# Layer 1's state mixer: chunk recurrence by one folded transition matrix per chunk, in place of three products per chunk

## The chip, the cores and the metric

One Trainium2 chip, one core of it. The metric is the device time of one execution in microseconds (us). A core has a matrix engine (TensorE, PE in the profile; its weight loads are PEld), a vector engine (DVE), a scalar engine (ACT), a general engine (POOL) and an engine that here only issues DMAs (SP). Each works through its own queue in order; they meet by semaphores that the compiler framework sets from the tiles that instructions read and write.

## The reference, cut to what matters

A backbone of two layers over 256 context and 256 latent tokens of 1024 features. Each layer is a feed-forward block, a token mixer and a feed-forward block. The mixer of layer 1 is the RWKV-7 recurrence, in both directions, over 16 heads of 64 features:

```
def step(s, inp):                        # s: state (64 x 64) of one head and direction
    r_t, w_t, k_t, v_t, kk_t, a_t = inp
    sa = einsum('ebhvk,ebhk->ebhv', s, -kk_t)
    s = s * w_t[..., None, :] + sa[..., None] * (kk_t * a_t)[..., None, :] + v_t[..., None] * k_t[..., None, :]
    return s, einsum('ebhvk,ebhk->ebhv', s, r_t)
s_fin, ys = lax.scan(step, s0, xs)
y = ys[:, 0] + jnp.flip(ys[:, 1], axis=0)
```

The context is scanned first, its readouts are not needed; the latent tokens are scanned from its final state. The summed readouts pass a normalization per head, a bonus and a gate, and the output projection.

## The kernel before, in words

The 512 tokens are cut into 8 chunks of 64 (0 to 3 context, 4 to 7 latent), the heads into four sets `s` of four heads: two feature tiles `q` of 128 features, each with two heads `par` in its two halves of 64 partitions. Directions are `d` = 0, 1. Within a chunk the recurrence becomes matrix algebra: a strictly triangular 64 x 64 matrix per chunk and head has to be inverted, and the state crosses the chunk by products.

The work on a set is written as generators:

- `prep` (L1513 ff., with `factors` and `scores`): rates, decay factors (L1596), the scaled operands `bk` and `zs` (L1601 to L1611), the scores as products (L1655, L1658), masked by DVE (L1660 to L1663), and transposes (L1669).
- `invert`: one transposition of all diagonal 32 x 32 blocks (tile `inva`, L1690), then an elimination of 31 steps on DVE, a multiplication (L1712) and a subtraction (L1715) each; in between `rebase` on POOL (L1681) multiplies `zs` by decays, and `modulation` computes a part of the next block's conditioning (L1756, L1765). At its end transpositions back (L1690) and two rounds of 32 x 32 products that join the blocks (L1733, L1741, evicted L1735, L1743). This end is called the inverse tail below.
- `recur`: the chain over 8 chunks, both directions in step. A chunk is a product of state and `zs` (L1798), an eviction by ACT (L1802), a product by the inverse (L1813), an eviction with sign (L1815), a product by `bt` (L1822) and on DVE the addition of the decayed state `f` (L1827; the decay is POOL's, L1793). The latent chunks add readouts (L1807, L1834, L1838 to L1843).
- `output` (normalization, bonus, gate; L1853 to L1903), and for the last set `early_o` and `late_o` (the output projection).

`together` interleaves generators by their share of steps done, and the order written so is the order in each queue. In `run`, set 0's inversion goes together with set 1's preparation, set 0's chain with set 1's inversion; then the chain of set `s` together with preparation and inversion of set `s + 1`; the last chain together with `early_o`. `output(s)` follows each chain. Tiles of one name share a buffer: a new one waits until the last reader of the old one is done.

Of the kernel before, what the change touches and what calls it, by code (L numbers as in the profile page):

```python
# [15 lines left out]
T = 512  # L16
# [1126 lines left out]
def consts_wkv():  # L1143


    p = np.arange(128)
    tau, j = p[:, None], np.arange(65)[None, :]
    cum = [((tau // L) == ch) * ((tau % L < j).astype(np.float32) - (tau % L < L // 2)) for ch in range(2)]
    blk = ((p[:, None] // L) == (p[None, :] // L)).astype(np.float32)
    oh = np.zeros((128, 8, 16), np.float32)  # L1150
    for f in range(8):
        oh[p, f, 2 * f + p // L] = 1.0
    s, t = (p % L)[:, None], np.arange(L)[None, :]
    masks = [(s < t), (s <= t)]
    return np.concatenate(cum + [np.eye(128) - blk / L, blk, oh.reshape(128, 128)] + masks, 1).astype(np.float32)
# [60 lines left out]
class Mixer1:  # L1216
# [15 lines left out]
    def run(self, epi):  # L1232
# [6 lines left out]
        with K.ctx_stack() as c2:  # L1239
# [12 lines left out]
            self.chain = [[self.cbank().rearrange("p (a b c) -> p a b c", a=4, b=2), K.bank((4, 2, 64), long=True)] for _ in range(2)]  # L1252
# [22 lines left out]
    def with_first(self, st, recur, prep, n):  # L1275

        def run():
            for i, _ in enumerate(prep):
                if i == 8:
                    self.loads(st)  # L1280
                    next(recur)
                yield
        return run(), n


    def consts(self):
        nc, mp, i, K = self.nc, self.mp, self.ins, self.K
        cw = mp.tile([128, 642], F32, name="cw")
# [4 lines left out]
        self.masks = cw[:, 514:642]  # L1293
# [174 lines left out]
    def values(self, pool):  # L1468

        K, nc = self.K, self.nc  # L1470
        for hf in range(2):
# [8 lines left out]
            st = pool.tile([128, 4 * T], F32, tag=f"sv{hf}", name="st")  # L1480
# [10 lines left out]
    def state(self, s, pool):  # L1491
# [76 lines left out]
    def factors(self, st, q, d, w2, a2):  # L1568
        K, nc, g = self.K, self.nc, self.late if d and self.late else self.g
        ZS, FX = st["ZS"], st["FX"]  # L1570

        for par in range(2):
            nc.gpsimd.memset(ZS[par][half(1 - par), d, q], 0.0)
# [25 lines left out]
        BK = g.tile([128, 8, 3, 64], F32, tag="bk", name="bk")  # L1599
        st["BK", d] = BK  # L1600
        nc.vector.scalar_tensor_tensor(out=BK[:, :, 0, :], in0=c8(TA[:, d]), scalar=0.5, in1=U[:, :, 1:65], op0=ALU.mult, op1=ALU.mult)  # L1601
        nc.vector.tensor_tensor(out=BK[:, :, 1, :], in0=c8(KD[:, d]), in1=U[:, :, 1:65], op=ALU.mult)
        nc.scalar.copy(out=BK[:, :, 2, :], in_=BK[:, :, 0, :])
        ctx = lambda z: z[:, d, q, 0:256].rearrange("p (c t) -> p c t", t=64)
        lat = lambda z: z[:, d, q, 256:768].rearrange("p (c x) -> p c x", x=128)
        c0, l0 = (slice(n, n + 4) for n in pos)
        for par in range(2):
            p = half(par)
            nc.gpsimd.tensor_tensor(out=lat(ZS[par])[p, :, 64:128], in0=c8(r)[p], in1=W[p, l0, 1:65], op=ALU.mult)
            nc.vector.tensor_tensor(out=lat(ZS[par])[p, :, 0:64], in0=c8(kk)[p, l0], in1=W[p, l0, 0:64], op=ALU.mult)  # L1610
            nc.vector.tensor_tensor(out=ctx(ZS[par])[p], in0=c8(kk)[p, c0], in1=W[p, c0, 0:64], op=ALU.mult)  # L1611
        yield

        fx = lambda n0, n1, i: nc.gpsimd.tensor_tensor(out=FX[:, d, q, n0:n1], in0=W[:, i:i + n1 - n0, 64], in1=U[:, i + 1:i + 1 + n1 - n0, 0],  # L1614
                                                       op=ALU.mult)
        if d == 0:
            fx(0, 7, 0)
        else:
            fx(0, 3, 4)
            fx(4, 7, 0)  # L1620
            nc.gpsimd.tensor_tensor(out=FX[:, d, q, 3:4], in0=W[:, 7:8, 64], in1=U[:, 0:1, 0], op=ALU.mult)
# [10 lines left out]
    def scores(self, st, q, d):  # L1632

        K, nc = self.K, self.nc
        ZS, BT, BR, FX, AB = (st[n] for n in ("ZS", "BT", "BR", "FX", "AB"))
        BK = st["BK", d]
        pos = [4, 0] if d else [0, 4]
        ctx = lambda z: z[:, d, q, 0:256].rearrange("p (c t) -> p c t", t=64)
        lat = lambda z: z[:, d, q, 256:768].rearrange("p (c x) -> p c x", x=128)

        bk = lambda c, par, p=slice(0, 128): BK[p, c, par:par + 2, :].rearrange("p a t -> p (a t)")
        u0 = d * 16 + q * 8

        def diag(par, u, ps):

            h0, h1 = (slice(64 * par + h, 64 * par + h + 32) for h in (0, 32))
            nc.scalar.copy(out=AB[h0, u:u + 4, :], in_=ps[h0, :, 0:64])
            nc.scalar.copy(out=AB[h1, u:u + 4, 0:32], in_=ps[h1, :, 32:64])

        mask = lambda a, x, n: self.masks[a, x].unsqueeze(1).to_broadcast([64, 4, n])  # L1650
        for par in range(2):
            p, o = half(par), half(1 - par)
            pl = K.bank((4, 128))
            for c in range(4):
                nc.tensor.matmul(pl[:, c, :], lhsT=bk(pos[1] + c, par), rhs=lat(ZS[par])[:, c, :], start=True, stop=True)  # L1655
            pc = K.bank((4, 128))
            for c in range(4):
                nc.tensor.matmul(pc[:, c, :], lhsT=bk(pos[0] + c, par), rhs=ZS[par][:, d, q, 64 * c:64 * c + 128], start=True, stop=True)  # L1658
            diag(par, u0 + 4, pl)
            nc.vector.tensor_tensor(out=lat(ZS[par])[o], in0=mask(o, slice(0, 128), 128), in1=pl[o], op=ALU.mult)  # L1660
            nc.vector.tensor_tensor(out=BR[p, d, q], in0=mask(p, slice(64, 128), 64), in1=pl[p, :, 64:128], op=ALU.mult)
            diag(par, u0, pc)
            nc.vector.tensor_tensor(out=ctx(ZS[par])[o], in0=mask(o, slice(0, 64), 64), in1=pc[o, :, 0:64], op=ALU.mult)  # L1663
            yield
        for par in range(2):
            p = half(par)
            pt = K.bank((7, 64))
            for c in range(7):
                nc.tensor.transpose(pt[:, c, :], bk(pos[c // 4] + c % 4, par, p), K.ident[p, p])  # L1669
            nc.scalar.copy(out=BT[par][:, d, q], in_=pt)  # L1670
            yield

    def rebase(self, st):

        for d in range(2):
            for q in range(2):
                for par in range(2):
                    p, z = half(par), st["ZS"][par]
                    for x, n, c in ((z[p, d, q, 64:256], slice(0, 3), 64), (z[p, d, q, 256:768], slice(3, 7), 128)):
                        x = x.rearrange("p (n c) -> p n c", c=c)  # L1680
                        self.nc.gpsimd.tensor_tensor(out=x, in0=x, in1=st["FX"][p, d, q, n].unsqueeze(2).to_broadcast([64, n.stop - n.start, c]), op=ALU.mult)  # L1681
                        yield

    @steps(38)
    def invert(self, st):
# [12 lines left out]
        for _, r1 in R:  # L1698
            nc.gpsimd.memset(AB[r1, :, 0:32], 0.0)
        yield  # L1700
        tmp = g.tile([128, 256], F32, tag="invt", name="invt")
        rebase, mods = self.rebase(st), self.modulation(5 + st["s"])
# [381 lines left out]
```

## Time and profile before

| | |
|---|---|
| time, three runs | 2631.14, 2634.19, 2635.12 us (median 2634.19) |
| the profiled execution | 2629.81 us, its span 2628.1 us |
| busy of the span | PE 93%, DVE 52%, ACT 42%, POOL 16% |
| state mixer from its first inversion to its last result | 1969.4 to 2411.7 us |

Times inside the span count from its start. "PEclk" is the clock that the chip granted to TensorE, as a share of full: 1.00 is 2.4 GHz, 0.50 is 1.2 GHz, and a figure between is a mean over a stretch that has both. A busy TensorE says that products are under way; at half clock the same products are busy for longer.

### The profile page before, as it was taken

To read this page: it belongs to the slowest core of one execution; us is meant where nothing else is said; L and a number is where in the kernel's file an instruction comes from. 1 tells how busy PE (TensorE), PEld (TensorE's weight loads), DVE (VectorE), ACT (ScalarE), POOL (GpSimd) and SP (SyncE) were. 2 spreads that over 40 slices of the span, in tenths; PEclk is the share of its full clock that TensorE was granted. 3 is DMA by queue.
4 is the path that set the end of the run, shared out by engine and by line. 5 is a ranking of instruction groups with operands and counts; after the bars stand their busy time and mean duration, and the time that the engine had idled before them with its cause. 6 is when DMAs were issued, how large, how long until landed. Compare 5 with 4: busy or idle time off the path is not lost. (4 is left out here: it accounts for less than half of the span.)

```text
span 2628.1 us, 39209 instructions
## 1 busy us (share of the span) xinstructions
PE 2441.9 (93%) x15555; PEld 1953.1 (74%) x15555; DVE 1363.5 (52%) x2406; ACT 1106.5 (42%) x2005; POOL 425.6 (16%) x546
## 2 busy tenths in 40 slices
PE   6999999998999999999999999997986888886998
PEld 5777777776777778777778888876875565655998
DVE  2322336775687473223244333356858867654555
ACT  4222225675565443222244222343644363534443
POOL 0000001033000110000010000023146273642000
PEclk9999999998999899999999999998998797967999
DMA  7545445343211234444444333323415312323553
GB/s 234 177 136 176 152 147 192 106 120 78 80 57 46 76 101 165 144 152 153 133 164 129 110 105 112 118 99 106 141 50 143 85 49 83 97 74 112 178 185 121
DMA packets 245476, 320.96 MB, mean 122 GB/s; under 512 B 34748, under 2 KB 186237, under 8 KB 245293
## 3 DMA queue, kind: packets, MB, share of 16 engines
q1 hardware_dynamic: 234157, 291.07, 35.3%
q0 software_dynamic: 7104, 20.05, 2.1%
q10 hardware_dynamic: 4032, 7.34, 0.8%
q8 instruction: 122, 2.00, 0.3%
q14 instruction: 61, 0.50, 0.1%
HBM read 301.77 MB, written 18.71 MB: 122 GB/s over the span
## 5 line engine op out<-in xcount | busy, mean ns | idle before, releaser
L62 DVE TENSOR_TENSOR wlo<-raw,whi 128x1024 fp32r<-128x1024 f32 x352 | 437.4, 1244 | 769.7 <-ACT whi L61 764.7
L420 PE MATMUL ps<-hth,whi 128*128 128x512 f32 (+1 forms) x1920 | 690.8, 362 | 28.2 <-ACT hth L397 13.1
L421 PE MATMUL ps<-htl,whi 128*128 128x512 f32 (+1 forms) x1920 | 687.3, 358 | 2.8 <-DVE htl L1344 2.8
L422 PE MATMUL ps<-hth,wlo 128*128 128x512 f32 (+1 forms) x1920 | 684.0, 357 | 0.0
L61 ACT CAST whi<-raw 128x1024 fp32r<-128x1024 f32 x352 | 368.9, 1049 | 680.2 <-PE ps L421 434.6
L420 PEld LDWEIGHTS ps<-hth,whi 128*128 128x128 f32 x1920 | 365.0, 191 | 101.8 <-issue 15.4
L421 PEld LDWEIGHTS ps<-htl,whi 128*128 128x128 f32 x1920 | 366.5, 191 | 56.7 <-issue 4.2
L422 PEld LDWEIGHTS ps<-hth,wlo 128*128 128x128 f32 x1920 | 366.3, 191 | 53.3 <-issue 2.8
L366 POOL TENSOR_SCALAR ss<-ss 128x1 f32<-128x1 f32 x42 | 22.2, 528 | 1441.1 <-ACT junk L364 1414.6
L420 PE MATMUL ps<-whi,g 128*128 128x512 f32 x616 | 244.0, 397 | 0.0
L421 PE MATMUL ps<-wlo,g 128*128 128x512 f32 x616 | 242.4, 394 | 0.0
L422 PE MATMUL ps<-whi,g 128*128 128x512 f32 x616 | 242.0, 394 | 0.0
L420 PEld LDWEIGHTS ps<-whi,g 128*128 128x128 f32 x616 | 116.3, 189 | 27.8 <-ACT whi L61 0.8
L422 PEld LDWEIGHTS ps<-whi,g 128*128 128x128 f32 x616 | 116.2, 189 | 26.9 <-DVE g L511 0.2
L421 PEld LDWEIGHTS ps<-wlo,g 128*128 128x128 f32 x616 | 116.3, 189 | 25.4
L510 ACT CAST g<-sg 128x512 fp32r<-128x512 f32 (+1 forms) x88 | 49.5, 565 | 109.2 <-DVE sg L507 109.2
L503 ACT ACTIVATE sg<-ps 128x512 f32<-128x512 f32 (+1 forms) x88 | 47.7, 542 | 102.6 <-PE ps L422 102.5
L507 DVE TENSOR_TENSOR sg<-sg,ps 128x512 f32<-128x512 f32 (+1 forms) x88 | 54.2, 618 | 39.1 <-PE ps L422 38.7
L1655 PE MATMUL ps<-zs,bk 128*128 128x128 f32 x256 | 42.2, 315 | 28.8 <-POOL fx L1614 17.5
L511 DVE TENSOR_TENSOR g<-sg,g 128x512 fp32r<-128x512 f32 (+1 forms) x88 | 54.4, 621 | 23.2 <-ACT g L510 23.2
L1655 PEld LDWEIGHTS ps<-zs,bk 128*128 128x128 f32 x256 | 36.9, 220 | 35.5 <-POOL fx L1614 18.6
L1712 DVE TENSOR_TENSOR invt<-inva,invx 128x110 f32<-128x110 f32 (+35 forms) x244 | 57.8, 275 | 1.9
(461 smaller groups left out, 3708.2 us busy)
## 6 DMA issues: line engine op xcount, KB each, us to landing
raw<-in_ffn_w_in_dram SPq DMA_DIRECT2D x176, 512.0 KB
raw<-in_ada_w_dram SPq DMA_DIRECT2D x112, 512.0 KB
raw<-in_ffn_w_out_dram SPq DMA_DIRECT2D x88, 512.0 KB
raw<-in_ev_w_in_dram SPq DMA_DIRECT2D x45, 512.0 KB
aw<-in_ada_w_dram SPq DMA_DIRECT2D x64, 256.0 KB
xres<-xt POOLq DMA_DIRECT2D x18, 512.0 KB, 3.1
ab<-acscr SPq DMA_DIRECT2D x16, 512.0 KB
raw<-in_ev_w_out_dram SPq DMA_DIRECT2D x16, 512.0 KB
```

The source lines that it names most:

```text
L61: parts = [K.nc.scalar.copy(out=hi, in_=raw), K.nc.vector.tensor_tensor(out=lo, in0=raw, in1=hi.bitcast(F32), op=ALU.subtract)]
L62: K.nc.vector.tensor_tensor(out=lo, in0=raw, in1=hi.bitcast(F32), op=ALU.subtract)]
L366: nc.gpsimd.tensor_scalar(out=ss, in0=ss, scalar1=D * 1e-6, scalar2=None, op0=ALU.add)
L420: mm(out, lhsT=wh, rhs=xh, start=start, stop=False)
L421: mm(out, lhsT=wh, rhs=xl, start=False, stop=False)
L422: mm(out, lhsT=wl, rhs=xh, start=False, stop=stop)
L503: nc.scalar.activation(out=t, in_=ps[q], func=AF.Silu)
L507: nc.vector.tensor_tensor(out=t, in0=t, in1=ps[q], op=ALU.mult)
L510: nc.scalar.copy(out=hi, in_=t)
L511: nc.vector.tensor_tensor(out=lo, in0=t, in1=hi.bitcast(F32), op=ALU.subtract)
L1655: nc.tensor.matmul(pl[:, c, :], lhsT=bk(pos[1] + c, par), rhs=lat(ZS[par])[:, c, :], start=True, stop=True)
L1712: nc.vector.tensor_tensor(out=t, in0=a[:, i0:i1, j:j + 1].to_broadcast([128, i1 - i0, w]), in1=x[:, j:j + 1, 0:w].to_broadcast([128, i1 - ...
```

## The change

For each chunk, head and direction the three products of the chain are multiplied out ahead of it. `fold` makes from the inverse, the scores and the operands one transition matrix (tile `GH`) and, for latent chunks, one readout matrix (`RR`), with the decay in a diagonal matrix `DR`. A chain step is then one product of the state (stacked with the chunk's values in 128 partitions) and `GH` (L1811), and a copy of the result into the next state, on DVE for direction 0 (L1812) and on ACT for direction 1. `rebase` and the POOL decays are gone, as `DR` holds them. Scores are computed per head with 64 rows instead of 128 with a zero half. `scan` runs folds 0 and 1, then direction 0's chain side by side with folds 2 and 3, then direction 1's chain with the readouts. The set's inversion and `scan` go one after the other, together with the next set's `prep`. The diff, with most removed lines cut (they stand in the kernel above), as well as some of `early_o`:

```diff
@@ run
-            nxt = self.state(1, sets[1])
-            recur, steps_left = self.recur(st)
-            together(self.invert(st), self.with_first(st, recur, *self.prep(nxt)))
+            self.chain, self.out = K.bank((2, 2, 64), long=True), K.bank((2, 4, 64), long=True)
             for s in range(4):
-                if s == 0:
-                    self.loads(nxt)
-                    together((recur, steps_left - 1), self.invert(nxt))
-                elif s < 3:
+                self.loads(st)
+                work = chain(self.invert(st), self.scan(st))
+                if s < 3:
                     nxt = self.state(s + 1, sets[(s + 1) % 2])
-                    together(self.recur(st), chain(self.prep(nxt), self.invert(nxt)))
-                    self.loads(nxt)
+                    together(work, self.prep(nxt))
                 else:
-                    together(self.recur(st), self.early_o(sets[0]))
+                    together(work, self.early_o(sets[0]))
                 self.output(st)
                 st = nxt
@@ loads
-                for par in range(2):
-                    for q in range(2):
-                        self.nc.sync.dma_start(out=tiles[h][half(1 - par), :, par, d, q],
-                                               in_=rows[:, q * 128:q * 128 + 128].rearrange("(n t) x -> t n x", t=64)[:, :, half(par)])
+                self.nc.sync.dma_start(out=tiles[h][64:128, :, d, :], in_=rows.rearrange("(n t) x -> t n x", t=64))
@@ factors
+        nc.vector.scalar_tensor_tensor(out=BK, in0=c8(TA[:, d]), scalar=0.5, in1=U[:, :, 1:65], op0=ALU.mult, op1=ALU.mult)
+        nc.vector.tensor_tensor(out=LK[:, x, 1:9, :], in0=c8(KD[:, d]), in1=U[:, :, 1:65], op=ALU.mult)
+        nc.gpsimd.tensor_tensor(out=DR[:, x, 7:11, :], in0=c8(r), in1=W[:, l0, 1:65], op=ALU.mult)
+        nc.vector.tensor_tensor(out=FE[:, 0:512].rearrange("p (c t) -> p c t", t=64), in0=c8(kk), in1=W[:, :, 0:64], op=ALU.mult)
+        nc.gpsimd.tensor_tensor(out=DR[:, x, 0:7, :], in0=self.one.unsqueeze(1).to_broadcast([128, 7, 64]),
+                                in1=FX[:, x, 0:7].unsqueeze(2).to_broadcast([128, 7, 64]), op=ALU.mult)
@@ scores
+        for n in range(8):
+            for p in heads:
+                if n < 4:
+                    mm(pc[p, n, :], lhsT=BK[p, pos[n], :], rhs=DR[p, n, :], start=True, stop=True)
+                else:
+                    mm(pl[p, n - 4, :].rearrange("p (a t) -> p a t", a=2), lhsT=BK[p, pos[n], :], rhs=DR[p, n:n + 4:3, :], start=True, stop=True)
+        nc.vector.tensor_tensor(out=RL[:, :, 64:128], in0=wide(self.upto), in1=pl[:, :, 64:128], op=ALU.mult)
...
+        nc.scalar.copy(out=AB, in_=pa)
...
+            nc.vector.tensor_tensor(out=z[:, :, 64:128], in0=wide(self.before), in1=pz[:, :, 64:128], op=ALU.mult)
@@ invert
-        rebase, mods = self.rebase(st), self.modulation(5 + st["s"])
+        mods = self.modulation(5 + st["s"])
...
-        X2 = g.tile([128, 32, 32], F32, tag="inva", name="invx2")
-        tr(X2.rearrange("p u j -> p j u"), x.rearrange("p i j -> p j i"))
+        X, XT = AB[:, :, 0:32], g.tile([128, 32, 32], F32, tag="inva", name="invxt")
+        tr(X.rearrange("p u j -> p j u"), x.rearrange("p i j -> p j i"))
+        tr(XT.rearrange("p u i -> p i u"), x)
         yield
-        for r0, r1 in R:
-            tr(AB[r1, :, 32:64].rearrange("p u i -> p i u"), x[r1])
-            tr(AB[r0, :, 0:32].rearrange("p u i -> p i u"), x[r0])
-            yield
@@ scan, fold, recur
+    @steps(24)
+    def scan(self, st):
+        for q in range(2):
+            yield from self.fold(st, q)
+        yield from side_by_side(self.recur(st, 0), itertools.chain(self.fold(st, 2), self.fold(st, 3)))
+        yield from self.recur(st, 1)
+        Y = st["Y"] = self.late.tile([128, 2, 4, 64], F32, tag="ysum", name="ysum")
+        self.nc.scalar.copy(out=Y, in_=self.out)
+
+    def fold(self, st, x):
+        XI = st["AB"][:, 8 * x:8 * x + 8]
...
+        for n in range(8):
+            for p in heads:
+                mm((pc[p, n] if n < 4 else pl[p, n - 4]), lhsT=XI[p, n, :], rhs=(RC[p, n] if n < 4 else RL[p, n - 4]), start=True, stop=True)
+        nc.scalar.mul(out=RC, in_=pc, mul=-1.0)
+        nc.scalar.mul(out=RL, in_=pl, mul=-1.0)
+        yield
...
+        def operands(par, n, second):
+            p = half(par)
+            o = ctx[par][:, n] if n < 4 else lat[par][:, n - 4] if n < 7 else lat[par][:, 3, 1, :]
+            if second:
+                r = DR[p, n, :] if n < 4 else DR[p, n:n + 4:3, :] if n < 7 else DR[p, 10, :]
+                for k, rows in ((0, half(0)), (1 + pos[n], half(1)))[::1 - 2 * par]:
+                    mm(o[rows], lhsT=LK[p, k, :], rhs=r, start=False, stop=True)
+            else:
+                r = RC[p, n, :] if n < 4 else RL[p, n - 4, :].rearrange("p (a t) -> p a t", a=2) if n < 7 else RL[p, 3, 64:128]
+                mm(o, lhsT=ZT[p, n, :], rhs=r, start=True, stop=False)
+        first, last = (0, 1, 2, 3), (7, 4, 5, 6)
+        for i, (n0, n1) in enumerate(zip(first + last, last + first)):
+            for second in range(2):
+                operands(0, n0, second)
+                operands(1, n1, second)
+            if i % 4 == 3:
+                yield
+        for par in (1, 0):
+            nc.vector.tensor_tensor(out=RR[:, par], in0=rev(self.readout.unsqueeze(1).to_broadcast([128, 4, 64])), in1=rev(lat[par][:, :, 1, :]), op=ALU.mult)
+            nc.scalar.copy(out=GH[:, par, 4:7, :], in_=lat[par][:, 0:3, 0, :])
+            nc.scalar.copy(out=GH[:, par, 0:4, :], in_=ctx[par])
+
+    def recur(self, st, d):
+        for n in range(8):
+            if n < 7:
+                rows = slice(0, 128) if n else half(1)
+                for h in range(4):
+                    mm(A[0:64, h, :], lhsT=GH(d, h, n, rows), rhs=SV[n][rows, d, h, :], start=True, stop=True)
+                (nc.scalar.copy if d else nc.vector.tensor_copy)(out=SV[n + 1][0:64, d], in_=A[0:64])
+            if n >= 4 and d:
...
+                            mm(self.out[half(par), q, c, :], lhsT=SV[m][:, e, h, :], rhs=RR(e, h, m - 4), start=(e == 0), stop=(e == 1))
+            yield
```

How the order moves, at two places. The first is DVE's queue around the opening transposition of an inversion, into the buffer `inva`. Before, in the queue up to inversion 2, the additions of set 1's chain (L1827) stand around it:

```order
L1663 TENSOR_TENSOR zs_16571<-cw,ps 64x256
L1827 TENSOR_TENSOR sv_15752<-chain,f_17119 64x128 x2
L1660 TENSOR_TENSOR zs_16572<-cw,ps 64x512
L1661 TENSOR_TENSOR br<-cw,ps 64x256
L1663 TENSOR_TENSOR zs_16572<-cw,ps 64x256
L1690 STREAM_TRANSPOSE inva<-ab 128x1024
L1827 TENSOR_TENSOR sv_15752<-chain,f_17128 64x128
L1712 TENSOR_TENSOR invt<-inva,invx 128x15
```

After, the same place at inversion 1, with the operations of `output` of set 0 (L1860, L1866, L1872) ahead of it:

```order
L1860 TENSOR_TENSOR ysum<-ps,gates 128x512
L1597 TENSOR_TENSOR lk<-kd,eu 128x512
L1866 TENSOR_SCALAR rr<-ps 128x8
L1612 SCALAR_TENSOR_TENSOR kd<-r,cols_10807,kd 128x256
L1872 TENSOR_TENSOR ysum<-ysum,ps 128x512
L1637 TENSOR_TENSOR rt<-cw,ps 128x4x64
L1665 STREAM_TRANSPOSE inva<-ab 128x1024
L1683 TENSOR_TENSOR invt<-inva,invx 128x15
```

The chain has left DVE's queue ahead of the inversion, and the whole output of the set before has come to stand there; the tile `gates` that it reads has the buffer of `inva`.

The second place is TensorE's queue in a chain step. Before, in set 0's chain, the three products of one chunk (`z` and `sv` are the evicted products) with conditioning work (L1765) between them:

```order
L1798 MATMUL chain<-sv_15115,zs_14267 64x64
L1765 MATMUL ps<-aw,cs 32x256 x2
L1813 MATMUL chain<-z_15834,ab 64x64 x4
L1813 MATMUL chain<-z_15843,ab 64x64 x4
L1765 MATMUL ps<-aw,cs 32x256 x2
L1822 MATMUL chain<-sv_15115,bt_14268 64x64
L1822 MATMUL chain<-sv_15115,bt_14269 64x64
```

After, in set 0's chain of direction 0, two chunks (L1811) with preparation (L1652, L1615) and a fold (L1768, L1785, L1782) between them:

```order
L1811 MATMUL ps<-sv_15019,zt 64x64 x4
L1652 MATMUL ps<-lk,fe 64x128 x8
L1768 MATMUL ps<-rt,ab 64x64 x8
L1768 MATMUL ps<-rt,ab 64x128 x8
L1811 MATMUL ps<-sv_15019,zt 64x64 x4
L1615 MATMUL ps<-kd,cw 128x256
L1785 MATMUL ps<-rt,zt 128x64
L1785 MATMUL chain<-rt,zt 128x64
L1782 MATMUL ps<-dr,lk 64x64 x2
L1782 MATMUL chain<-dr,lk 64x64 x2
```

A chunk is one group of products now instead of three, and a fold's products alternate between two forms.

## Rows read from the trace of the kernel before

**Rows 1.** The page's busy times by engine.
```profile
PE 2441.9 (93%) x15555; PEld 1953.1 (74%) x15555; DVE 1363.5 (52%) x2406; ACT 1106.5 (42%) x2005; POOL 425.6 (16%) x546
```

**Rows 2.** Windows: stretch; PE, PEld, DVE, ACT, POOL busy; PEclk, DMA, GB/s.
```profile
1883.00:1969.40 86.40, 79.10 (x449) 64.96 (x448) 52.26 (x77) 43.53 (x93) 42.69 (x56) 0.96 0.18 54
1969.40:2054.60 85.20, 61.42 (x624) 46.31 (x623) 73.18 (x188) 40.45 (x95) 47.69 (x61) 0.80 0.42 121
2054.60:2106.60 52.00, 45.52 (x696) 28.37 (x696) 45.45 (x159) 19.12 (x54) 14.48 (x28) 0.80 0.34 93
2106.60:2225.00 118.40, 97.80 (x1247) 73.63 (x1248) 83.10 (x236) 57.44 (x165) 69.24 (x99) 0.84 0.25 70
2225.00:2334.80 109.80, 91.61 (x1109) 71.23 (x1110) 77.83 (x225) 54.01 (x150) 59.78 (x77) 0.80 0.27 82
2334.80:2411.70 76.90, 67.49 (x650) 47.14 (x649) 20.42 (x54) 26.41 (x76) 29.35 (x41) 0.84 0.25 83
```

**Rows 3.** Groups by line, 1700 to 2400 us: busy, mean ns | idle before.
```profile
L1802 ACT COPY z<-chain 128x128 f32<-128x128 f32 x64 | 16.6, 269 | 52.6 <-PE chain L1798 45.9 <-DVE invx L1715 3.4 <-issue 1.9
L1815 ACT ACTIVATE sv<-chain 64x128 f32<-64x128 f32 x128 | 34.7, 271 | 29.5 <-PE chain L1813 16.0 <-PE ps L1807 10.2 <-POOL f L1793 0.6
L1827 DVE TENSOR_TENSOR sv<-chain,f 64x128 f32<-64x128 f32 x96 | 27.6, 288 | 38.0 <-ACT sv L1815 14.8 <-PE chain L1822 12.2 <-ACT yo L1967 4.7
L1681 POOL TENSOR_TENSOR zs<-zs,fx 64x192 f32<-64x192 f32 x64 | 49.1, 785 | 36.8 <-PE ps L1658 30.6 <-issue 4.1 <-DMA o<-oscr 1.0
L1601 DVE SCALAR_TENSOR_TENSOR bk<-ta,eu 128x512 f32<-128x512 f32 x16 | 12.8, 797 | 0.7 <-ACT eu L1596 0.7
L1629 ACT COPY bonus<-ps 128x256 f32<-128x256 f32 x8 | 3.0, 376 | 3.0 <-PE ps L1628 2.7
```

**Rows 4.** DVE's timeline in inversion 2: start, duration, operation.
```profile
2172.16 1.93 DVE L1690 STREAM_TRANSPOSE inva<-ab 128x1024 f32<-128x1024 f32 x1
...
2197.66 0.47 DVE L1712 TENSOR_TENSOR invt<-inva,invx 128x120 f32<-128x120 f32 x2
2198.05 0.47 DVE L1715 TENSOR_TENSOR invx<-invx,invt 128x120 f32<-128x120 f32 x2
2198.43 0.46 DVE L1712 TENSOR_TENSOR invt<-inva,invx 128x105 f32<-128x105 f32 x2
...
2209.18 2.01 DVE L1690 STREAM_TRANSPOSE invx<-invx 128x1024 f32<-128x1024 f32 x1
```

**Rows 5.** TensorE's timeline, forms of products (rows*columns of the array used).
```profile
1961.32 1.05 PE L1655 MATMUL ps<-zs,bk 128*128 128x128 f32 x8
...
2042.61 0.88 PE L1733 MATMUL ps<-invx,ab 32*32 32x32 f32 x42
2043.41 0.65 PE L1669 MATMUL ps<-ident,bk 64*128 64x64 f32 x7
2043.99 1.79 PE L1733 MATMUL ps<-invx,ab 32*32 32x32 f32 x86
...
2129.92 0.45 PE L1798 MATMUL chain<-sv,zs 128*64 128x64 f32 x8
...
2133.21 0.68 PE L1813 MATMUL chain<-z,ab 64*64 64x64 f32 x16
...
2142.67 0.89 PE L1669 MATMUL ps<-ident,bk 64*128 64x64 f32 x14
```

**Rows 6.** TensorE's timeline, one round of the inverse tail, sets 1 and 3.
```profile
2096.01 2.21 PE L1733 MATMUL ps<-invx,ab 32*32 32x32 f32 x128
...
2321.91 3.62 PE L1733 MATMUL ps<-invx,ab 32*32 32x32 f32 x128
```

**Rows 7.** Timeline of the last output and the mixer's end.
```profile
2392.00 0.63 POOL L1843 TENSOR_TENSOR ysum<-ysum,yt 128x128 f32<-128x128 f32 x1 [0.47 <-DVE yt L1842]
...
2402.23 0.69 DVE L1897 TENSOR_TENSOR ysum<-ysum,ew 128x512 f32<-128x512 f32 x1
...
2411.05 0.69 DVE L1982 TENSOR_TENSOR yo<-yo,ps 128x512 f32<-128x512 f32 x1 [0.71 <-PE ps L422]
```

**Rows 8.** Windows around inversion 3's end, as in Rows 2.
```profile
2302.00:2308.00 6.00, 1.17 (x20) 0.85 (x22) 5.85 (x27) 0.27 (x1) 1.23 (x3) 0.71 0.09 38
...
2320.00:2332.00 12.00, 11.47 (x251) 9.32 (x251) 8.67 (x7) 7.69 (x15) 8.43 (x6) 0.50 0.29 79
2332.00:2344.00 12.00, 12.00 (x99) 7.99 (x95) 0.23 (x1) 5.57 (x12) 1.73 (x1) 0.50 0.34 114
2346.00:2352.00 6.00, 6.00 (x58) 3.88 (x56) 1.54 (x5) 3.06 (x8) 5.77 (x5) 1.00 0.07 20
```

More of the change, by code (lines that the diff above doesn't have):

```diff
@@ L1273, in run @@
             self.w_o(epi)
[L1275 to L1281, printed above, removed]
-                yield
-        return run(), n
     def consts(self):
         nc, mp, i, K = self.nc, self.mp, self.ins, self.K
-        cw = mp.tile([128, 642], F32, name="cw")
+        cw = mp.tile([128, 834], F32, name="cw")
         nc.sync.dma_start(out=cw, in_=i["wkv_consts"])
@@ L1292, in consts @@
         self.oh = cw[:, 386:514].rearrange("p (f r) -> p f r", f=8)
-        self.masks = cw[:, 514:642]
+        self.upto, self.before, self.one, self.readout = (cw[:, c:c + 64] for c in (578, 642, 706, 770))
         rows = mp.tile([104, 128], F32, name="rows1")
@@ L1568, in factors @@
     def factors(self, st, q, d, w2, a2):
[L1569 to L1573, printed above, removed]
+        K, nc, g = self.K, self.nc, self.g
+        own = self.late if d and self.late else g
+        x, FX, LK, DR = 2 * d + q, st["FX"], st["LK"], st["DR"]
         TH = g.tile([128, 4, 128], F32, tag="th", name="th")
@@ L1598, in factors @@
             yield
[L1599 to L1605, printed above, removed]
@@ L1616, in factors @@
[L1616 to L1621, printed above, removed]
+        BK = own.tile([128, 8, 64], F32, tag="bk", name="bk")
+        FE = own.tile([128, 544], F32, tag="fe", name="fe")
+        st["BF", x] = BK, FE
+        nc.gpsimd.memset(FE[:, 512:544], 0.0)
+        nc.vector.scalar_tensor_tensor(out=BK, in0=c8(TA[:, d]), scalar=0.5, in1=U[:, :, 1:65], op0=ALU.mult, op1=ALU.mult)
@@ L1644, in diag @@
[L1644 to L1663, printed above, removed]
-            yield
@@ L1665, in scores @@
[L1665 to L1682, printed above, removed]
@@ L1684, in invert @@
-    @steps(38)
+        K, nc, mm = self.K, self.nc, self.nc.tensor.matmul
+        x = 2 * d + q
+        LK, DR, ZT, RC, RL = (st[n][:, x] for n in ("LK", "DR", "ZT", "RC", "RL"))
+        AB = st["AB"][:, 8 * x:8 * x + 8]
+        BK, FE = st["BF", x]
+        pos = [(n + 4) % 8 if d else n for n in range(8)]
+        wide = lambda m: m.unsqueeze(1).to_broadcast([128, 4, 64])
+        heads = [half(par) for par in range(2)]
+        pc, pl = K.bank((4, 64)), K.bank((4, 128))
+        for n in range(8):
[4 more added lines that the diff above has]
+                    mm(pl[p, n - 4, :].rearrange("p (a t) -> p a t", a=2), lhsT=BK[p, pos[n], :], rhs=DR[p, n:n + 4:3, :], start=True, stop=True)
@@ new lines, in scores @@
+        nc.scalar.copy(out=AB, in_=pa)
+        yield
+        for n0 in (0, 4):
+            pz = K.bank((4, 128))
+            for n in range(n0, n0 + 4):
+                for p in heads:
+                    mm(pz[p, n - n0, :].rearrange("p (a t) -> p a t", a=2), lhsT=FE[p, 64 * pos[n]:64 * pos[n] + 64], rhs=LK[p, 0:2 + pos[n]:1 + pos[n], :],
+                       start=True, stop=True)
+            z = ZT[:, n0:n0 + 4]
+            nc.scalar.copy(out=z[:, :, 0:64], in_=pz[:, :, 0:64])
+            nc.vector.tensor_tensor(out=z[:, :, 64:128], in0=wide(self.before), in1=pz[:, :, 64:128], op=ALU.mult)
+            yield
@@ L1685, in invert @@
+    @steps(37)
     def invert(self, st):
@@ L1736, in invert @@
             yield
+        for r0, r1 in R:
+            nc.scalar.copy(out=AB[r1, :, 32:64], in_=X[r1])
+            nc.gpsimd.memset(AB[r0, :, 32:64], 0.0)
         for b in range(2):
@@ L1942, in weight @@
[L1942 to L1944 removed]
+                blocks.extend(old(late, t, 32, 32) for t in ("inva", "invx"))
+            hi, lo = blocks[2 * k], [spare, old(g, "bk", 8, 64)] if k == 7 else blocks[2 * k + 1]
+            nc.scalar.copy(out=hi, in_=raw)
+            if k == 7:
+                for j, l in enumerate(lo):
+                    c = slice(512 * j, 512 * j + 512)
+                    nc.gpsimd.tensor_tensor(out=l, in0=raw[:, c], in1=hi[:, c].bitcast(F32), op=ALU.subtract)
+            else:
+                nc.gpsimd.tensor_tensor(out=lo, in0=raw, in1=hi.bitcast(F32), op=ALU.subtract)
+                lo = lo[:, 0:512], lo[:, 512:1024]
```

184 lines of the change are left out of this document (64 added, 120 removed).

## The prediction

> **What bounds the kernel now.** I read the page's busy times first. TensorE is busy 93% of the span and every other engine far less [rows 1], so the kernel as a whole is bound by TensorE. That is an average, and the change sits in one stage, so next I cut the state mixer into six stretches at the inversions' boundaries [rows 2]: preparation of set 0; inversion 0 with preparation 1; the chain of set 0 beside inversion 1; twice "chain of one set beside preparation and inversion of the next"; last the chain of set 3 with the output. From the first transposition of inversion 0 (1969.4 us) to the mixer's end (2411.7) it takes 442.3 us. In all of these stretches TensorE is busy 72 to 88%, at a granted clock of 0.80 to 0.84 of full. No engine is full: each stretch is several dependent chains laid beside each other, and its length is set by the sum of two of them.
>
> Then the grouped lines [rows 3] show what the chain consists of. Each chunk has three products one behind the other, and the wait in front of each eviction is for exactly the product before it (the two ACT copies and the DVE addition of the chain). POOL's rebasing takes 49.1 us beside it. The vector queue [rows 4] shows the other chain, the elimination: 31 steps of two dependent operations, one step each 0.77 us at 120 elements (2197.66 to 2198.43).
>
> **The change part by part.**
>
> Busy work, first. TensorE loses the 128-row score products, at 1.05 us for eight instructions [rows 5], and the three-part chain; it gains 64-row products in larger number: 2348 mixer products become 3276, and with the form prices of rows 5 I get some +27 us of TensorE time over the mixer. By the same counting DVE loses 93 us, POOL 118 (the rebasing's 49.1 among them) and ACT 36. None of these three is the bound as a whole, so this relief is worth only what it takes out of a chain. I therefore walk the chain.
>
> What the order shows: before, the transposition that opens the next inversion stands among the additions of the running chain, and waits for nothing but its own scores. After, it writes the buffer "inva", which the output of the set before uses as "gates" until its last operation, so it stands behind that output. Inversion, folds, chain and output of one set thus become one serial loop, four times; preparation of the next set fills the gaps.
>
> *Front* (preparation 0, 86.4 us [rows 2]): per quarter TensorE loses 4.8 us and gains 6.0, while masks and rebasing on other engines go. I take 0, with -6 to +6.
>
> *Elimination.* The two operations of a step take 0.47 each, of which 0.77 remains in time since they overlap at their ends [rows 4]; the shorter and longer steps scale to about 23.5 us for the 31. Opening transposition 1.93; the two transpositions at its end 2 x 2.01 [rows 4]. On the same queue stand, interleaved, the preparation's operations of the next set: 12 or so of 0.4 to 0.8 us (512 elements 0.80 [rows 3]), 9 us. With 1.5 us of stalls: 40 us. For set 0 half as much preparation again stands there, and the stretch of before shows the vector engine busy 73.2 of its 85.2 us [rows 2]: 48. For set 3 there is no preparation: 30.
>
> *Inverse tail.* Two times 64 small products; 128 instructions take 2.21 us at full clock and 3.62 at half [rows 6]. Two rounds with evictions: 6.5 us. Before, this took 16 us in set 2 (2209.2 [rows 4] to 2225.0 [rows 2]), as five transpositions stood ahead.
>
> *Folds.* One fold per direction and feature tile. First 16 products, 32 instructions: half with 64 columns at 0.68/16 = 0.043, half with 128 at 0.89/14 = 0.064 [rows 5], 1.7 us. Two ACT evictions, 0.38 for 256 elements [rows 3] and by proportion 0.6 for 512: 1.0. Then 16 products with 128 outputs (32 instructions, 2.2 us) and 32 of 64 x 64 (64 instructions, 24 of them of 128 columns, 3.5 us), in alternation. A switch between product forms costs 0.07 to 0.13 us beyond the work itself: 42 products of 32 x 32 at 2.21/128 = 0.017 [rows 6] need 0.73, and the next form starts 0.80 after; the seven transpositions behind need 7 x 0.064 = 0.45, and the next form starts 0.58 after [rows 5]. A fold has 16 switches: 16 x 0.11 = 1.8. Last the copies, four on ACT, 1.5. Sum 11.7, two folds a little overlapped: 23. Folds 2 and 3 run beside the first direction's chain; both fill TensorE, 24.
>
> The Trainium skill ("TensorEngine Tiling (Array Packing)", Tiling Modes, Key Properties) says that changing the tiling mode, not just the tile, drains TensorE, and that tiles operate independently. The gaps of 0.07 to 0.13 us at the changes of form agree with the first [rows 5]. By that rule the 1.8 us a fold stay lost however well the products overlap, an estimate of 29 us over sixteen folds; if no drain were paid, the sum below would come out 3 us below before, at no change.
>
> *Chain.* The second direction's chain has nothing beside it but readouts. A step is four products (eight instructions; the nearest row, eight alternating over column halves, takes 0.45 [rows 5]) and one copy of 256 elements, 0.38 [rows 3]: a floor of 0.83. Above it, before's stretch of 52.0 us [rows 2] holds some 23 products of set 0's chain one behind another, 2.26 each with inversion work beside. I take 1.25, near the floor since little else stands there: 7 x 1.25, and readouts and final copy 3.7: 12.5 us.
>
> *Output.* Before it takes from the last addition into its input (2392.00) to the end of its last vector operation (2402.9) [rows 7] 10.9 us; with preparation beside it 11.5.
>
> Sum. Sets 1 and 2: 40 + 6.5 + 23 + 24 + 12.5 + 11.5 = 117.5 each. Set 0: 125.5. Set 3, with early output work beside it and less preparation: 30 + 6.5 + 21 + 20 + 11 + 10 = 98.5, and the late part 9 (2402.9 to 2411.7 [rows 7]): 107.5. Together 468 against 442.3: **+25.7 us**. By set: before, the first two stretches take 137.2, then 118.4, 109.8 and 76.9; after 125.5, 117.5, 117.5 and 107.5. Set 0 gains; the last set loses 30, because its elimination was hidden in set 2's chain and now stands open.
>
> Loads of the state: 16 DMAs of 64 x 4 x 256 in place of 64 small ones, issued a full inversion before the chain reads them, so at nothing; if that cover were gone, the first chain step would wait a few microseconds per set.
>
> Against the profiled execution's 2629.81 us that is 2655.5; it lies 4.4 below the median of the runs, so the forecast is **2660 us**.
>
> **The clock.** After a stretch in which TensorE was busy 1.17 of 6 us the granted clock is at 0.50, 1.2 GHz, and stays there while TensorE is busy 11.47 and 12.00 of 12; later it is 1.00 [rows 8]. This is the largest unknown. Each after-loop has a stretch of elimination in which TensorE does only the preparation's products. If the half clock then holds into the folds, a fold's 7.4 us of products grow by 3.62/2.21 [rows 6] to 12.1; for folds 0 and 1 of all four sets that is 8 x 4.7 = 38 us on top of the forecast, 2698. The sum takes the full clock, as a set's inverse tail did in 2.21 us, and the range holds the other.
>
> **The rivals.**
>
> *B, faster.* The denser TensorE work keeps its full clock (before 0.80 to 0.84 over these stretches [rows 2]), elimination has no stalls, since POOL's rebasing and the additions are gone from it, and row halves overlap fully. Per set: four folds at 10 in place of 11.7, -7; tail -1.5, stalls -3, output -1, together -12.5; over four sets -50, with -4 in front -54 from the forecast: **2606**. For it: 93 us less vector work and two products fewer in every step. Against: TensorE gets more work and switches.
>
> *C, much slower.* Of the 128-column products with 64 rows, halves do not overlap: 0.131 an instruction, as the 128-row ones (1.05/8 [rows 5]), in place of 0.064. That is 52 instructions in a fold, 208 in a set, x 0.067 = 14 us a set, 56 in all, of which preparation's gaps hide a little: **2705**. It decides if pairs of these products start more than 0.1 us apart. It is told apart from half clock by the granted clock in the rows.
>
> *D, no change.* The serial loop costs what it saves: one chain step of 1.25 in place of three products, exactly paid by the open elimination of set 3. **2634**. For it: up to set 2 the two schedules differ by 5 us in my sum (365.4 before, 360.5 after). Against: it needs 20 us of set 3's 30 to be hidden by its early output work.
>
> **How the numbers follow.** Forecast A (2640 to 2690) 0.47; B 0.30; C 0.13; D 0.10. What a measurement can tell from no change is 0.2%, 5 us. Faster: B and a little of D and A, 0.32; same 0.10; slower: A and C, 0.58. The range reaches from just beyond B to just beyond C: 2600 to 2712; A's own is 2640 to 2690.
>
> **What would show it.** In the changed kernel's rows the opening transposition of inversions 1 to 3 should wait for POOL or the output, four loops should be some 118 us long, a fold 11 to 12 us, a chain step alone 1.2 to 1.3. A loop below 108 us, or an opening transposition that stands early, makes it B; a fold over 14 us at full clock, C. The forecast is wrong at its root if the elimination takes over 50 us or under 33.

## The result

The changed kernel took 2735.21 us in the median (2724.65 to 2745.02) against 2632.66: a ratio of 1.039, interval 1.035 to 1.043. Slower was forecast, but at 2660; the time lies 23 us above the range. The profiled execution has a span of 2735.9 us against 2628.1; of the 107.8 us between them the stretch from inversion 0 to the mixer's end has 107.0 (549.3 against 442.3).

The windows of the changed kernel by the stages of the prediction, set 1 first (elimination, inverse tail, folds 0 and 1, folds 2 and 3 beside direction 0's chain, direction 1's chain, output), then tail and folds of set 3; columns as in [rows 2]:

```profile
2114.54:2154.84 40.30, 25.06 (x324) 13.97 (x323) 36.30 (x141) 12.16 (x27) 13.20 (x16) 0.84 0.43 133
2154.84:2165.08 10.24, 10.24 (x287) 9.39 (x289) 1.65 (x1) 6.20 (x10) 2.08 (x3) 0.50 0.01 3
2165.08:2192.17 27.09, 27.09 (x356) 20.18 (x354) 2.53 (x6) 8.66 (x21) 2.53 (x4) 0.75 0.02 5
2192.17:2221.02 28.85, 28.85 (x459) 22.50 (x459) 8.76 (x18) 7.38 (x19) 3.06 (x6) 0.85 0.05 16
2221.02:2239.70 18.68, 18.68 (x160) 13.11 (x156) 3.38 (x6) 9.14 (x21) 3.06 (x3) 0.71 0.16 38
2239.70:2251.60 11.90, 8.46 (x67) 6.38 (x66) 5.10 (x9) 2.41 (x7) 7.45 (x7) 0.74 0.36 90
...
2415.10:2425.51 10.41, 10.41 (x262) 8.72 (x262) 1.65 (x1) 5.46 (x8) 1.89 (x2) 0.50 0.01 3
2425.51:2460.40 34.89, 34.89 (x266) 24.50 (x263) 1.27 (x3) 6.13 (x13) 4.84 (x3) 0.55 0.00 1
2460.40:2489.80 29.40, 29.40 (x345) 21.43 (x340) 4.61 (x11) 5.81 (x15) 0.00 (x0) 0.88 0.01 1
```

Summed over the four sets, by the same windows (us):

| stage | forecast | measured | difference |
|---|---|---|---|
| elimination | 158 | 167.3 | +9.3 |
| inverse tail | 26 | 41.2 | +15.2 |
| folds 0 and 1 | 90 | 116.7 | +26.7 |
| folds 2 and 3, chain 0 | 92 | 113.1 | +21.1 |
| chain 1 | 48.5 | 55.7 | +7.2 |
| output and end | 53.5 | 55.4 | +1.9 |

The stages together exceed the sum by 81 us. Some 63 of them stand in the tails and the folds, where TensorE is recorded busy 100% of the stretch, at a granted clock of 0.50 to 0.92; the excess of direction 1's chain is set 1's, at 0.71. A view of three microseconds each through folds 0 and 1 of set 1 shows when the clock goes (the first number in brackets counts TensorE's instructions):

```profile
2171.00:2174.00 3.00, 3.00 (x50) 2.03 (x50) 0.27 (x1) 0.37 (x1) 0.00 (x0) 1.00 0.00 0
...
2177.00:2180.00 3.00, 3.00 (x36) 2.42 (x32) 0.00 (x0) 1.08 (x3) 0.20 (x1) 1.00 0.00 0
2180.00:2183.00 3.00, 3.00 (x22) 1.75 (x21) 0.00 (x0) 0.00 (x0) 0.00 (x0) 0.59 0.02 5
2183.00:2186.00 3.00, 3.00 (x30) 2.45 (x30) 0.00 (x0) 0.00 (x0) 0.00 (x0) 0.50 0.00 0
...
2189.00:2192.00 3.00, 3.00 (x26) 2.04 (x24) 0.84 (x2) 1.01 (x3) 0.00 (x0) 0.50 0.01 3
```

The half clock of the tail doesn't simply last: it is back at 1.00 through fold 0 and then falls in the middle of fold 1, with TensorE recorded busy throughout. A busy share of 100% therefore does not say how many products pass: three microseconds at the full clock held 50 instructions in one slice and 36 in another.

### The profile page after: what moved, and what is told of

Its sections match the earlier page's. It is cut to its first block, busy times and chain, and to the rows that moved or that the text cites. A ratio compares the mean times of both kernels' runs of the same rounds, so it can differ in the third digit from the quotient of the medians.

```text
span 2735.9 us, 42498 instructions
## 1 busy us (share of the span) xinstructions
PE 2543.6 (93%) x17635; PEld 2019.7 (74%) x17635; DVE 1280.8 (47%) x2214; ACT 1077.6 (39%) x1821; POOL 315.5 (12%) x359
## 5 line engine op out<-in xcount | busy, mean ns | idle before, releaser
L421 PEld LDWEIGHTS ps<-htl,whi 128*128 128x128 f32 x1920 | 368.8, 192 | 55.7 <-issue 4.2
L1785 PE MATMUL chain<-rt,zt 64*128 64x128 f32 (+1 forms) x256 | 70.4, 361 | 0.0
L1785 PE MATMUL ps<-rt,zt 64*128 64x64 f32 x256 | 63.2, 332 | 0.0
```

Of the source, the lines that this page charges most:

```text
L421: mm(out, lhsT=wh, rhs=xl, start=False, stop=False)
L1785: mm(o, lhsT=ZT[p, n, :], rhs=r, start=True, stop=False)
```

## The experiments

Four theories. **1**: TensorE runs dry in the elimination, its clock falls, and tail and folds run at half clock on the serial path. **2**: the folds' small products and their changes of form are dear at any clock. **3**: the serial order alone costs it. **4**, formed after the first four runs: the alternation of forms within a fold is itself what lowers the clock. (A form is the part of the array that a product uses, rows*columns, as in 64*128 or 64*64.) Each ratio is to runs of the kernel before that stood beside the experiment; their medians lie between 2633 and 2639 us, and a difference in us between two experiments carries that much.

**e1_warm**: products without use keep TensorE busy during the elimination.

```diff
+            if j >= (12 if st["s"] == 3 else 18):
+                for _ in range(2):
+                    self.warm(x[:, j:j + 1, 0:32])
...
+        for _ in range(6):
+            self.warm(x[:, 31:32, 0:32])
...
+    def warm(self, row):
+        self.nc.tensor.matmul(<chain bank, 256 columns>, lhsT=self.K.ident, rhs=row.to_broadcast([128, 8, 32]), start=True, stop=True)
```

> Changed kernel with extra products whose results are never read: two 128 x 256 products after each late elimination step, each reading a row of the inverse that is final by then, and six at its end. Theory 1 (TensorE runs dry in the elimination, its granted clock falls to 0.50, and the inverse tail and the first folds then run at half clock on the serial path): tail 10.3 to about 6.5 us, folds 0 and 1 from 27 (35 in set 3) to about 23, some 35 us off in all, about 2700 us, although TensorE does more. Theory 2 (the folds' small products and their changes of form are dear at any clock) and theory 3 (the serial order alone): no gain, 2735 to 2745 us.

Measured 2759.47 us, ratio 1.046 (1.043 to 1.049), slower than the changed kernel. Its windows: elimination, tail and first folds of set 1, both pairs of folds of set 2, tail of set 3:

```profile
2128.30:2169.85 41.55, 39.86 (x383) 25.00 (x382) 34.89 (x137) 13.13 (x26) 6.51 (x12) 0.99 0.43 129
2169.85:2179.20 9.35, 7.64 (x294) 7.18 (x295) 3.39 (x4) 5.70 (x11) 6.03 (x8) 0.89 0.01 4
2179.20:2205.88 26.68, 26.68 (x354) 19.77 (x353) 2.52 (x6) 7.84 (x19) 0.99 (x3) 0.76 0.02 5
...
2320.30:2341.46 21.16, 21.16 (x355) 16.03 (x353) 2.53 (x6) 7.60 (x19) 0.45 (x2) 1.00 0.03 9
2341.46:2366.83 25.37, 25.37 (x459) 19.89 (x459) 7.65 (x17) 8.21 (x23) 5.44 (x7) 1.00 0.13 44
...
2438.86:2445.90 7.04, 6.97 (x266) 5.82 (x265) 0.00 (x0) 4.56 (x8) 1.89 (x2) 1.00 0.01 2
```

The time lies above what any theory gave. The elimination kept 0.99, and set 1's folds still fell to 0.76. So theory 1 holds for the tail: at full clock it takes 7.04 us in set 3, in place of 10.41. In set 1 the stretch is only 0.9 us shorter, as TensorE waits there 1.43 us for POOL's `dr`, in a preparation product that stands ahead of the folds:

```profile
2176.82 0.88 PE L1632 MATMUL ps<-dr,bk 64*64 64x64 f32 x16 [1.43 <-POOL dr L1606]
```

In three sets of four the folds lost their clock with a warm elimination ahead of them. Only in set 2 did it last, and there two pairs of folds take 21.16 + 25.37 = 46.5 us: the forecast's 47, at the clock that it had taken. The extra products cost more than they gained: the four eliminations took 197 us in place of 167.

**e2_group**: eight changes of form in a fold in place of sixteen.

```diff
-        for i, (n0, n1) in enumerate(zip(first + last, last + first)):
-            for second in range(2):
-                operands(0, n0, second)
-                operands(1, n1, second)
+        for i in range(4):
+            for second in range(2):
+                for n0, n1 in ((first[i], last[i]), (last[i], first[i])):
+                    operands(0, n0, second)
+                    operands(1, n1, second)
...
```

> Changed kernel with each fold's products taken in groups of four and eight instead of two and four: 8 changes of form a fold in place of 16, nothing else. Theory 2: 16 folds x 8 changes x 0.11 us = 14 us off, about 2721 us. Theories 1 and 3: at most 5 us off, 2730 to 2735.

Measured 2662.53 us, ratio 1.009 (1.006 to 1.013): 73 us off, five times theory 2's 14. The two pairs of folds of set 1, then the start of fold 0's alternating products on TensorE and what comes behind them:

```profile
2138.96:2157.55 18.59, 18.59 (x357) 16.02 (x355) 2.23 (x6) 7.91 (x20) 2.53 (x4) 0.88 0.02 7
2157.55:2179.04 21.49, 21.49 (x460) 18.68 (x459) 7.90 (x18) 7.00 (x20) 3.58 (x6) 1.00 0.07 21
...
2143.81 0.32 PE L1785 MATMUL ps<-rt,zt 64*128 64x64 f32 x1
...
2148.19 1.02 PE L1645 MATMUL ps<-fe,bk 64*32 64x64 f32 x57
```

27.09 and 28.85 became 18.59 and 21.49, the clock 0.75 and 0.85 became 0.88 and 1.00, with the same products and the elimination before them untouched (39.20 us at 0.84). The pass over the alternating products takes 4.38 us at the full clock (2143.81 to 2148.19), against 6.03 in the changed kernel (shown under e5): 0.21 us for each of the eight changes saved, with no product added or taken away. No theory so far had the clock's part; it gave theory 4.

**e3_overlap**: the changed algebra in the order of before.

```diff
+            together(self.invert(st), self.prep(nxt))
...
-                work = chain(self.invert(st), self.scan(st))
-                if s < 3:
+                if s == 0:
+                    together(self.scan(st), self.invert(nxt))
+                elif s < 3:
                     nxt = self.state(s + 1, sets[(s + 1) % 2])
-                    together(work, self.prep(nxt))
+                    together(self.scan(st), chain(self.prep(nxt), self.invert(nxt)))
...
```

> The changed algebra in the order of before: preparation and inversion of set s + 1 are laid beside the folds and the chain of set s (one accumulator moves into the free half of the chain's bank, so that the conditioning keeps its own). Theory 3 (the loss is the open elimination): inversions are hidden again, 2610 to 2660 us. Theory 1: TensorE has folds to do during the elimination, so the clock holds as well; same number, and the granted clock in the folds at 0.85 or more. Theory 2: the folds cost what they cost, 2690 us or more.

Measured 2679.87 us, ratio 1.016 (1.014 to 1.018): between theories 2 and 3. The order is worth 55 us here, and the folds keep costing. Theory 1 asked for 0.85 in the folds: the first folds of set 0, with an elimination beside them, ran at 0.50 (2040.4 to 2053.6).

**e4_serial_before**: the algebra of before in the serial order (`chain(self.invert(st), self.recur(st))` beside `self.prep(nxt)`).

> The algebra of before in the serial order of the changed kernel: inversion then chain of one set, beside the preparation of the next, then its output. Theory 3: the order is what costs, so this loses as well, 2680 to 2735 us. Theory 2: the order is harmless, 2630 to 2655 us. Theory 1: a loss as theory 3, with tail at 0.50 clock, but less than the changed kernel's, since no TensorE-bound folds follow: 2660 to 2700.

Measured 2672.08 us, ratio 1.013 (1.011 to 1.014), +35 us. The order costs the old algebra as well, about a third of the whole loss. The time lies below theory 3's range and inside theory 1's, but not for theory 1's reason: the first round of the inverse tail had the full clock in three sets of four (2.21 us in set 1) and 0.50 in set 3 alone.

**e5_split**: each fold product with 128 outputs becomes two of 64 x 64, so that a fold has one form; 16 products more in each.

```diff
-                mm(o, lhsT=ZT[p, n, :], rhs=r, start=True, stop=False)
+                for rows in heads:
+                    mm(o[rows], lhsT=ZT[p, n, rows], rhs=r, start=True, stop=False)
```

> Changed kernel with each of the folds' products with 128 outputs issued as two products of 64 x 64, in the old alternation: no change of form within a fold, but 16 more products in each. Theory 4 (the alternation of forms makes TensorE's work so thin that the granted clock falls inside the folds): clock in folds 0 and 1 at 0.87 or more in the sets 0 to 2, two folds in 17 to 19 us in place of 27, about 2665 us as with grouping. Theory 2 in its plain form (a fold costs its instructions and its changes of form, the clock has other reasons): 256 changes fewer at 0.1 us against 512 instructions more at 0.043, 2725 to 2735 us.

Measured 2645.41 us, ratio 1.005 (1.004 to 1.007): 90 us off by adding work, and below what either theory gave. One fold's pass over these products, on TensorE, in the changed kernel (first products, last ones, and what comes next):

```profile
2168.67 0.32 PE L1785 MATMUL ps<-rt,zt 64*128 64x64 f32 x1
2168.68 0.32 PE L1785 MATMUL chain<-rt,zt 64*128 64x64 f32 x1
...
2169.04 0.27 PE L1782 MATMUL ps<-dr,lk 64*64 64x64 f32 x2
...
2174.50 0.28 PE L1782 MATMUL chain<-dr,lk 64*64 64x128 f32 x2
2174.70 1.10 PE L1645 MATMUL ps<-fe,bk 64*32 64x64 f32 x64
```

and in the split kernel:

```profile
2146.29 0.27 PE L1786 MATMUL ps<-rt,zt 64*64 64x64 f32 x2
...
2149.06 0.39 PE L1782 MATMUL chain<-dr,lk 64*64 64x128 f32 x4
2149.37 0.82 PE L1645 MATMUL ps<-fe,bk 64*32 64x64 f32 x44
```

6.03 us with 96 instructions against 3.08 with 128, both at the full clock. In that sense the alternating work is thin. Its windows for the folds of set 1, ahead of them folds 2 and 3 of set 0:

```profile
2046.20:2065.45 19.25, 19.25 (x519) 17.39 (x521) 8.00 (x18) 7.25 (x19) 3.58 (x6) 1.00 0.08 24
...
2141.49:2157.89 16.40, 16.28 (x421) 15.01 (x419) 2.44 (x6) 8.12 (x21) 2.52 (x4) 0.87 0.03 8
2157.89:2177.14 19.25, 19.25 (x519) 17.39 (x521) 8.01 (x18) 7.25 (x19) 3.58 (x6) 1.00 0.08 24
```

All fold stages together take 141.1 us in place of 229.8. Of the 88.7, 16 x 2.95 = 47 are the changes of form at the full clock. The clock has most of the other 42. What it costs, two equal halves of a pass in the changed kernel show, in fold 1 and fold 3 of set 1:

```profile
2185.95:2191.01 5.06, 5.06 (x50) 3.22 (x49) 0.84 (x2) 1.07 (x3) 0.00 (x0) 0.50 0.01 2
2202.13:2205.11 2.98, 2.98 (x50) 2.03 (x48) 0.84 (x2) 1.00 (x3) 0.00 (x0) 1.00 0.03 5
```

Over all eight fold windows the changed kernel spent 97 us at 0.50, the split one 14 (twice length times 1 - PEclk). At 5.06 for 2.98 these 83 us would have been 49 at the full clock: an estimate of 34 us for the clock, which leaves 8 open.

**e6_overlap_group** and **e7_overlap_split**: both changes with the overlap order.

> Both at once: the folds' products grouped, and preparation and inversion of the next set beside folds and chain. If order (-55 us) and fold form (-73) are separate losses, they add: about 2607 us, faster than the kernel before. If the overlap won its 55 us only because it gave the thin folds company, little is left of it: 2640 to 2660.

> The overlap order with the folds' products in 64 x 64 form alone. Theory 4: as the grouped overlap within 10 us. If 64 x 64 products beside other forms bring back the changes of form: 15 us or more above it.

Measured 2636.59 us, ratio 1.002 (0.9995 to 1.004), and 2623.89, ratio 0.997 (0.995 to 0.999). The gains don't add: -55 and -73 became -99. With folds in one form the order is worth 21 us (2645.41 to 2623.89), so more than half of e3's 55 hangs on the folds' two forms. That the overlap gives the thin folds company is a reading of this; no run shows it by itself. e6 fell between its two expectations; e7 is 13 us under e6, just beyond theory 4's 10. e7 is below the kernel before by 0.3%, but its mixer takes 443.5 us, as before; the stretch ahead of inversion 0 ends at 1962.0 us there and at 1970.1 in e1, with the same code up to that point, so its gain is not located.

**e8_forms**: the split kernel with the changes of form put back by products of 4 columns.

```diff
+                if not second:
+                    mm(self.spare, lhsT=ZT[0:64, n0, :], rhs=RC[0:64, 0, 0:4], start=True, stop=True)
```

> The split kernel (64 x 64 products only, 2645 us) with the changes of form put back and nothing else: behind each of the eight first groups of a fold one product with 128 outputs and 4 columns, whose result is never read. Theory 4 (it is the changes of form that thin TensorE's work and take the clock): 16 changes a fold are back, two folds at 25 us or more again, clock in folds 0 and 1 at 0.80 or less, 2700 to 2740 us. If the length of the 128-output products was dear and not the changes: 128 short products in all, under 15 us, below 2660.

Measured 2768.24 us, ratio 1.050 (1.047 to 1.052): 123 us more than the split kernel (117 if each is taken against its own runs of the kernel before), for 128 tiny products, and above theory 4's range. Folds 2 and 3 of set 0, then both pairs of set 1:

```profile
2056.44:2083.56 27.12, 27.12 (x556) 22.55 (x555) 8.40 (x18) 7.44 (x20) 3.58 (x6) 1.00 0.05 17
...
2164.18:2192.36 28.18, 28.18 (x453) 23.73 (x451) 2.53 (x6) 8.52 (x21) 2.53 (x4) 0.73 0.02 4
2192.36:2223.97 31.61, 31.61 (x556) 26.25 (x555) 8.40 (x18) 7.53 (x20) 3.59 (x6) 0.83 0.05 15
```

Set 0's folds 2 and 3 stayed at 1.00, as in the split kernel: 27.12 against 19.25, 0.25 us for each of 32 changes, the small products among it. In set 1 the clock fell as well, and so it did in seven of the eight fold stages: folds 0 and 1 of the four sets stand at 0.84, 0.73, 0.67 and 0.50, against 0.92, 0.87, 0.86 and 0.90 in the split kernel (theory 4 asked for 0.80 or less). Direction 1's chain, behind them, fell to 0.72, 0.66 and 0.61 in sets 0 to 2, from 1.00. Taking changes out by grouping (e2) or splitting (e5) raised the clock, putting them back lowered it: the changes of form are shown as the cause. Short products without a change of form were not run, so the 0.25 us holds the product as well; e2's 0.21 does not. By what in the thinned work the clock falls stays open, and so does why it sometimes holds.

**e9_pairs**: split folds in a third order.

```diff
+                if s % 2 == 0:
+                    together(self.scan(st), self.invert(nxt))
+                elif s == 1:
+                    nxt = self.state(2, sets[0])
+                    together(self.scan(st), self.prep(nxt))
...
+                if s == 1:
+                    nxt = self.state(3, sets[1])
+                    together(self.invert(st), self.prep(nxt))
```

> The 64 x 64 folds in a third order: inversion 0 beside preparation 1, chain 0 beside inversion 1, chain 1 beside preparation 2, inversion 2 beside preparation 3, chain 2 beside inversion 3, chain 3 beside the early output work. Each elimination of an odd set lies under folds and chain, and no preparation stands ahead of an inversion in one stretch as in e7. From stretches of the split kernel: 64 + 58 + 12 + 60 + 12 + 50 + 58 + 12 + 64 = 390 us for the mixer against 442: 2575 to 2600 us. If the elimination beside folds is slowed by evictions on its own queue as in e7: 2600 to 2625.

Measured 2618.80 us, ratio 0.993 (0.991 to 0.995): 0.7% faster than the kernel before, in the upper of the two expected ranges. Windows from inversion 0 to inversion 1, to output 0, to inversion 2, and to inversion 3:

```profile
1968.20:2037.20 69.00, 53.19 (x921) 37.41 (x920) 55.87 (x160) 31.80 (x67) 29.08 (x40) 0.90 0.51 147
2037.20:2104.40 67.20, 63.59 (x1186) 48.60 (x1187) 34.40 (x144) 22.61 (x51) 6.73 (x7) 0.80 0.27 76
2104.40:2199.30 94.90, 83.97 (x1567) 68.80 (x1569) 35.65 (x64) 44.24 (x104) 36.30 (x41) 0.93 0.18 48
2199.30:2252.20 52.90, 41.66 (x782) 29.26 (x783) 46.25 (x152) 24.19 (x53) 17.45 (x24) 0.90 0.37 104
```

The mixer is 432.0 us long, 10 below before, and the profiled span 11 (2616.8 against 2628.1). Chain 0 and elimination 1 together took 67.2, not 58, and chain 1 with preparation 2 and the two outputs 94.9, not 84.

## Why the prediction was wrong

**The direction and the loop were right.** Inversions 1 to 3 open behind the output of the set before, as forecast (two of them shown):

```profile
2114.54 1.98 DVE L1665 STREAM_TRANSPOSE inva<-ab 128x1024 f32<-128x1024 f32 x1 [0.65 <-POOL ysum L1873]
...
2251.60 1.99 DVE L1665 STREAM_TRANSPOSE inva<-ab 128x1024 f32<-128x1024 f32 x1 [0.64 <-POOL ysum L1873]
```

The elimination of sets 1 and 2 took 40.3 and 40.4 us (40 forecast), the output 11.9 and 12.2 (11.5). A chain step with little beside it takes 1.13 to 1.21 (1.25), as four products of set 2's direction 1 show by their starts:

```profile
2362.23 0.68 PE L1811 MATMUL ps<-sv,zt 128*64 128x64 f32 x8 [0.46 <-ACT sv L1812]
...
2363.44 0.62 PE L1811 MATMUL ps<-sv,zt 128*64 128x64 f32 x7
...
2364.57 0.50 PE L1811 MATMUL ps<-sv,zt 128*64 128x64 f32 x5
...
2365.71 0.50 PE L1811 MATMUL ps<-sv,zt 128*64 128x64 f32 x5
```

**The step that failed is "The sum takes the full clock".** The text named the clock as the largest unknown, and had an end for it, 2698. But it bounded it by the elimination, for folds 0 and 1 alone. The half clock also held in the four tails (+15.2), in part of folds 2 and 3, and in set 1's direction 1 chain (18.68 us at 0.71; the split kernel's set 1 took 14.00 at 1.00). The folds spent 97 us at 0.50, some 40 us more than at the full clock by the estimate under e5. e1 shows that a warm elimination does not keep the clock in three sets of four; e2, e5 and e8 show that the folds' own alternation of forms takes it. For the tails e1 shows the cause: with TensorE kept busy through the elimination, set 3's ran at 1.00 and took 7.04 us, near the 6.5 of the sum. The comparison was uneven from the start: it set stages priced at the full clock against 442.3 us that were measured at 0.80 to 0.84.

**The price of a change of form was about half of what it is**: 0.11 taken; measured 0.18 (6.03 - 3.08 over 16, which also pays for the split kernel's 16 products more), 0.21 (e2) and 0.25 (e8, with its small product). The products were priced too high in turn: 5.7 us of them in a pass, where the whole pass with its changes took 6.03. That a fold at full clock came out right is luck, two errors that cancelled. The estimate of 29 us for all 256 changes is 47 to 63 at these prices, without counting the clock. It stood beside what the Trainium skill ("TensorEngine Tiling (Array Packing)", Tiling Modes, Key Properties) says, that a change of tiling mode drains TensorE; e2, e5 and e8 agree with it so far that every change costs time.

**The elimination of sets 0 and 3** was taken 4 us too short each (52.3 and 34.3 measured); the cause stays open. The relief of the other engines, counted from preparation 0 to the mixer's end, came near: DVE 81 us less (93), POOL 110 (118), ACT 29 (36). One reading was off and entered no sum: ahead of DVE's addition L1827 the longest wait in [rows 3] is for ACT's eviction (14.8 us), the product's is second (12.2).

**Rivals.** B's premise, that denser work keeps the clock, failed: the work was more, but thinner. Its overlap of row halves held, and that speaks against C. C gave the nearest number, 2705, for a reason that the trace refutes: the first products of a fold are 32 instructions, half of them with 128 columns, and take at the full clock

```profile
2176.38 1.56 PE L1768 MATMUL ps<-rt,ab 64*64 64x64 f32 x32
```

while at C's 0.131 the sixteen alone would need 2.1. D needed 20 us of set 3's elimination hidden; it stood open for 34.3.

## What to carry to other kernels

Keep a run of small products in one form: two 64 x 64 products in place of one 64 x 128 were much the cheaper choice between other 64 x 64 products. Read the granted clock beside the busy share in every stretch of small products, since a TensorE that is 100% busy there can be at half clock by its own doing. Price algebra and order apart before both are changed together: here the new algebra in the new order lost 3.9% with mixed forms and 0.5% in one form, and in one form it gained 0.3% in the order of before and 0.7% in a third order.

## What the runs showed of the hardware

Changes between 64*128 and 64*64 products cost 0.18 to 0.25 us each at the full clock. A stretch with 32 of them in 27 us went to 0.50 of the clock with TensorE recorded busy 100% (from about 2180.5 to 2192), and not always: folds 2 and 3 of e8's set 0 stayed at 1.00, and so did both pairs of folds of e1's set 2. The same half pass of small products took 5.06 us at 0.50 and 2.98 at 1.00, the same round of 128 small products of the tail 3.62 [rows 6] and 2.21. Two 64*64 products in place of one 64*128 made the pass shorter between other 64*64 products, 3.08 us for 6.03.
